# Down projection by seven products of quarters (Strassen's scheme, the form with 15 sums), with the sums of weight quarters made in DRAM by adding DMAs

## Chip, cores and metric

The kernel runs on one core of a Trainium2 chip. The metric is the device time of one execution in microseconds (us), as the median of several runs. Engine names: PE is TensorE, DVE is VectorE, ACT is ScalarE, POOL is GpSimd, SP is SyncE, which here only issues DMAs.

## What is computed

The reference is one decoder layer on 512 tokens of width 1024 in float32: three token mixers, their gated merge, and then a gated feed-forward block. Only the last lines matter here:

```python
D_FF = ((8 * D_MODEL // 3 + 127) // 128) * 128      # 2816
...
h = rmsnorm(x, norm2_g[l])
u = causal_dwconv(h @ ffn_up[l], ffn_conv_w[l], ffn_conv_b[l])
u_gate, u_val = jnp.split(u, 2, axis=-1)
x = x + (jax.nn.gelu(u_gate) * u_val) @ ffn_down[l]
...
return rmsnorm(x, final_g)
```

The down projection is the product with `ffn_down`, a matrix of 2816 rows and 1024 columns.

## The kernel before

Every float32 operand of a matmul is split into a high part (rounded to fp32r by an ACT cast) and a low part (the remainder, by a DVE subtraction), and each product is made of three matmuls: high by high, high by low, low by high. All matmuls are issued at line 77.

The feed-forward block has two stages. In the **up stage** (lines 933 to 949) 44 weight tiles of 128 columns, gate and value in turn, are multiplied with the normalised input; 24 matmuls of 512 columns each. After each pair `glu` (line 921) runs the convolution, the GELU and the gating on DVE and ACT and leaves the result as a pair of pages (`acth`, `actl`), 128 features by 512 tokens. There are 22 such row tiles (`NF`).

In the **down stage** (lines 967 to 1001) the kernel goes over the two halves of the output columns (`hf`). In each, four PSUM banks (`psd`) hold the four token tiles, and 11 weight loads of two row tiles each (`dn_t`) run past them: for each row tile, four token tiles, three matmuls. The activations are stationary, 128 by 128, and the weights move, 128 by 512. The last 2 loads of the first half and the last 4 of the second (`NLAST`) are kept in pages (`load_wp`, line 105), so that the token tiles end one after the other. At the end of a token tile DVE adds the bank to the residual (line 993), ACT makes the sum of squares (line 994), DVE multiplies with the gain (line 996), and in the second half `finish` (line 959) scales with the reciprocal root, whose power is made on POOL (line 867), and stores the result from SP and ACT.

Weights come through `load_w` (line 93): a DMA from SP to a `wr` buffer, the cast to `wh` on ACT (line 101), the remainder `wl` on DVE (line 102). There are three buffers of each of the three kinds. The engines run their instructions strictly in the order in which they were issued to them; a scheduler that simulates a timeline writes that order when the program is built, so it need not be that of the source. Pages (`pg`) are 128 by 512 floats, 58 of them (`NPG`), beside 22 of the second pool (`ag`).

Of the kernel before, what the change touches and what calls it, by code (L numbers as in the profile page):

```python
# [10 lines left out]
F32 = mybir.dt.float32  # L11
F32R = mybir.dt.float32r
AF = mybir.ActivationFunctionType
ALU = mybir.AluOpType
ADD, SUB, MUL, MAX = ALU.add, ALU.subtract, ALU.mult, ALU.max

S = 512
D = 1024
KD = D // 128
NT = S // 128  # L20
DFF = 2816
NF = DFF // 128
EPS = 1e-6
NEG = -1.0e30
NPG = 58
NAT = 22
NWARM = 9
WCOL = 1088
NLAST = (2, 4)
LAM_INIT = 0.2  # L30
GELU_C = 0.7978845608028654
GELU_A = 0.044715
# [14 lines left out]
def build(ctx, tc, A, out):  # L47
# [13 lines left out]
    def pg(name, dt=F32):  # L61
        return page.tile([128, 512], dt, name=name, tag="pg")
# [4 lines left out]
    def bank(name):  # L67
        return psm.tile([128, 512], F32, name=name, tag="mm")

    def abank(name):  # L70
        return psa.tile([128, 512], F32, name=name, tag="at")
# [4 lines left out]
    def mm(ps, a, b, start, stop):  # L76
        PE.matmul(ps, a, b, start=start, stop=stop)  # L77
# [15 lines left out]
    def load_w(ap, n, parts=1):  # L93
        raw = wpool.tile([128, WCOL], F32, name="wr", tag="wr")
        hi = wpool.tile([128, WCOL], F32R, name="wh", tag="wh", bufs=3)
        lo = wpool.tile([128, WCOL], F32R, name="wl", tag="wl", bufs=3)
        with tc.high_priority() if hp[0] else ExitStack():
            for p in range(parts):
                c = slice(n // parts * p, n // parts * (p + 1))
                nc.sync.dma_start(raw[:, c], ap[:, c])  # L100
                SC.copy(hi[:, c], raw[:, c])  # L101
                V.tensor_sub(lo[:, c], raw[:, c], hi[:, c])  # L102
        return hi, lo

    def load_wp(ap):

        raw = wpool.tile([128, WCOL], F32, name="wr", tag="wr")
        nc.sync.dma_start(raw[:, :1024], ap)
        res = []
        for p in range(2):  # L110
            c = slice(512 * p, 512 * (p + 1))
            h = pg("wph", F32R)
            l = pg("wpl", F32R)
            SC.copy(h, raw[:, c])
            V.tensor_sub(l, raw[:, c], h)
            res.append((h, l))
        return res

    def split(src, name, al=None):
        al = al or pg  # L120
        h = al(name + "h", F32R)
        l = al(name + "l", F32R)
        SC.copy(h, src)  # L123
        V.tensor_sub(l, src, h)
        return h, l
# [738 lines left out]
    def rsqrt_act(s1, s0, nm):  # L864
        y = small([128, 1], nm + "y")
        V.tensor_scalar(y, s1, 1.0 / D, s0, op0=MUL, op1=ADD)  # L866
        G.tensor_tensor(y, y, mhalf[:, 0:1], op=ALU.pow)  # L867
        return y
# [43 lines left out]
    def up(wt, name):  # L912
        ps = bank(name)
        mm3(ps, [wt(k) + (h2h[k], h2l[k]) for k in range(KD)])
        return ps

    def up_half(ps, wt, hf):
        c = slice(256 * hf, 256 * (hf + 1))
        mm3(ps[:, c], [wt(k) + (h2h[k][:, c], h2l[k][:, c]) for k in range(KD)])

    def glu(c, psg, psv):
        ug = conv(psg, [col("fw", 44 * j + c) for j in range(3)], col("fb", c))
        uv = conv(psv, [fwh[:, 22 * j + c:22 * j + c + 1] for j in range(3)], fwh[:, 66 + c:67 + c])
        q = pg("gq")
        SC.activation(q, ug, AF.Square)
        V.tensor_scalar(q, q, GELU_A, 1.0, op0=MUL, op1=ADD)
        V.tensor_mul(q, q, ug)
        SC.activation(q, q, AF.Tanh, scale=GELU_C)  # L928
        V.scalar_tensor_tensor(ug, q, 1.0, ug, op0=ADD, op1=MUL)  # L929
        V.tensor_mul(ug, ug, uv)  # L930
        acts.append(split(ug, "act", ag if c < 10 else None))

    acts = []
    order = [i for c in range(NF) for i in (c, NF + c)]
    first_w[1] = up_w(order[1])
    first_w[2] = up_w(order[2])
# [7 lines left out]
    for n in range(3, 2 * NF):  # L944
        w, nxt = nxt, up_w(order[n + 1]) if n + 1 < 2 * NF else None
        ps = up(w, "psu")
        if n % 2:
            glu(n // 2, prev, ps)
        prev = ps

    ss3 = const.tile([128, NT, 2], F32, name="ss3")
    NP = NF // 2
    fgp = []
    for hf in range(2):
        fg = pg("fg")
        nc.sync.dma_start(fg, A["final_g"][512 * hf:512 * (hf + 1)].partition_broadcast(128))
        fgp.append(fg)

    def finish(t):
        z = rsqrt_act(ss3[:, t, 1:2], ss3[:, t, 0:1], "rs3")  # L960
        o = [pg("of") for _ in range(2)]
        SC.activation(o[1], x1[t][1], AF.Copy, scale=z)
        V.tensor_scalar(o[0], x1[t][0], z, None, op0=MUL)
        nc.sync.dma_start(out[128 * t:128 * (t + 1), 0:512], o[0])
        SC.dma_start(out[128 * t:128 * (t + 1), 512:1024], o[1])

    for hf in range(2):
        pst = [bank("psd") for _ in range(NT)]
        held = []

        def dmm(t, k, wh, wl):
            ts_ = slice(128 * t, 128 * (t + 1))
            ah, al = acts[k]
            for j, (a, b) in enumerate(((al, wh), (ah, wl), (ah, wh))):
                mm(pst[t], a[:, ts_], b, k == 0 and j == 0, k == NF - 1 and j == 2)

        nl = NLAST[hf]
        nxt = load_w(A["dn_t"][hf, 0], 1024)
        for p in range(NP - nl):
            hi, lo = nxt  # L980
            if p + 1 < NP - nl:
                nxt = load_w(A["dn_t"][hf, p + 1], 1024)
            else:
                held = [(p, load_wp(A["dn_t"][hf, p])) for p in range(NP - nl, NP)]
            for kk in range(2):
                for t in range(NT):
                    dmm(t, 2 * p + kk, hi[:, 512 * kk:512 * (kk + 1)], lo[:, 512 * kk:512 * (kk + 1)])
        for t in range(NT):
            xx = x1[t][hf]
            for p, w in held:  # L990
                for kk in range(2):
                    dmm(t, 2 * p + kk, *w[kk])
            V.tensor_add(xx, pst[t], xx)
            SC.activation(abank("sqj"), xx, AF.Square, accum_out=ss3[:, t, hf:hf + 1])
            xg = pg("xg")
            V.tensor_mul(xg, xx, fgp[hf])
            x1[t][hf] = xg
            if not hf:
                V.tensor_scalar(ss3[:, t, 0:1], ss3[:, t, 0:1], 1.0 / D, EPS, op0=MUL, op1=ADD)
            else:  # L1000
                finish(t)


def _bucket():
# [12 lines left out]
def layout(i):  # L1017
    f = {k: np.asarray(v) for k, v in i.items()}
    x = f["x"][0]
    w = f["w_in"][0]  # L1020
    o = np.cumsum([0, 1024, 1024, 512, 512, 512, 512, 512, 512, 8, 3072])
    part = [w[:, o[j]:o[j + 1]] for j in range(10)]
    cat = np.concatenate
    A = {}
    A["x"] = np.ascontiguousarray(x)
    A["xT"] = np.ascontiguousarray(x.T.reshape(8, 128, 512).transpose(1, 0, 2))
    A["w_t"] = _tiles(cat([part[0], part[1], part[2], part[3], part[5], part[6], part[9]], axis=1))
    A["wv_d"] = _tiles(part[4], 2, 512)
    A["wv_f0"] = _tiles(cat([part[7][:, :256], part[8]], axis=1), 4, 264)
    A["wv_f1"] = _tiles(part[7][:, 256:], 4, 256)  # L1030
    A["br_r"] = _tiles(f["w_br_rnn"][0])
    for n, w in (("br_d", "w_br_diff"), ("br_f", "w_br_fox")):
        t = _tiles(f[w][0], 4).reshape(4, 2, 128, 512).transpose(0, 2, 1, 3)
        A[n] = np.ascontiguousarray(t).reshape(4, 128, 1024)
    A["w_out"] = np.ascontiguousarray(f["w_out"][0])
    A["up_t"] = _tiles(f["ffn_up"][0])
    d = f["ffn_down"][0].reshape(NF // 2, 2, 128, 2, 512).transpose(3, 0, 2, 1, 4)
    A["dn_t"] = np.ascontiguousarray(d).reshape(2, NF // 2, 128, 1024)
    A["rg_t"] = np.ascontiguousarray(cat([f["rg_w_r"][0], f["rg_w_i"][0]], axis=2))

    def c(v):
        return v.reshape(-1, 128).T

    A["cols"] = np.ascontiguousarray(cat([
        c(f["norm1_g"][0]), c(f["rnn_conv_w"][0]), c(f["rnn_conv_b"][0]), c(f["rg_b_r"][0]), c(f["rg_b_i"][0]),
        c(f["rg_a"][0]), c(f["gate_b"][0]), c(f["norm2_g"][0]), c(f["ffn_conv_w"][0]), c(f["ffn_conv_b"][0]),
        c(f["diff_subln_g"][0])], axis=1))
    A["final_g"] = np.ascontiguousarray(f["final_g"])
    A["rows"] = cat([f["fox_b_f"][0], f["diff_lq1"][0], f["diff_lk1"][0], f["diff_lq2"][0],
                     f["diff_lk2"][0]])  # L1050
    A["rel_bias"] = np.ascontiguousarray(f["rel_bias"])
    A["onehot"] = (np.arange(32)[:, None] == _bucket()[::-1][None, :]).astype(np.float32)
    p = np.arange(128)
    A["mask"] = np.where(p[None, :] <= p[:, None], 0.0, NEG).astype(np.float32)
    A["flip"] = (p[None, :] == 127 - p[:, None]).astype(np.float32)
    return A
# [1 line left out]

# [10 lines left out]
```

## Time and profile before

| | |
|---|---|
| median of 3 runs | 936.99 us (936.97 to 938.68) |
| the profiled execution | 938.8 us, of which the span from first to last instruction is 937.0 us |
| mean granted clock of TensorE | 0.998 of full speed |
| busy time in the span | PE 925.1 us (99%), DVE 633.8 (68%), ACT 482.7 (52%), POOL 95.9 (10%) |
| matmuls of the down stage | 528, from 810.72 us on |

A busy PE only says that a matmul was in flight; the pace is read from the starts of consecutive matmuls. An engine off the critical path costs nothing while it is idle. The profiled execution is one run among several, so a forecast that is summed from its rows is set against its own 938.8 us.

### The profile page before, as it was taken

How to read it: one execution, taken by the hardware profiler on the slowest of the kernel's cores; microseconds unless marked ns; L12 is line 12 of the kernel's file. 1: busy time of each engine (PE TensorE's matmuls, PEld its weight loads, DVE VectorE, ACT ScalarE, POOL GpSimd, SP SyncE). 2: the span in 40 equal slices, each digit the busy share in tenths (PEclk: the TensorE clock that was granted, in tenths of full speed). 3: DMA queues.
4: the chain of work that ended last, by engine and by line, in shares of the span. 5: the costliest groups of instructions: out<-in, count | busy, mean ns of one | idle time of the engine just before them, and what ended most of it. 6: DMA issues, size and time to landing. Idle time of an engine off the chain costs nothing.

```text
span 937.0 us, 11825 instructions
## 1 busy us (share of the span) xinstructions
PE 925.1 (99%) x4363; PEld 771.6 (82%) x4363; DVE 633.8 (68%) x1215; ACT 482.7 (52%) x835; POOL 95.9 (10%) x77
## 2 busy tenths in 40 slices
PE   9999999999999999999999999999999999999997
PEld 6788888998887887888888889888888888888885
DVE  5679797787759778857656734877777777633323
ACT  7577777755465657444454434554444454422212
POOL 0021310200121126321100000000000000000000
PEclk9999999999999999999999999999999999999999
DMA  9522222222322221322245510322322322334112
GB/s 328 173 93 96 80 90 69 69 91 91 107 85 84 97 96 57 105 98 97 73 142 167 189 43 1 113 90 91 111 90 91 111 91 91 113 103 144 45 68 90
DMA packets 31577, 95.14 MB, mean 102 GB/s; under 512 B 3824, under 2 KB 5364, under 8 KB 31520
## 3 DMA queue, kind: packets, MB, share of 16 engines
q1 hardware_dynamic: 30944, 93.35, 29.4%
q10 hardware_dynamic: 576, 1.05, 0.3%
q8 instruction: 34, 0.56, 0.2%
q14 instruction: 23, 0.19, 0.1%
HBM read 92.26 MB, written 2.12 MB: 101 GB/s over the span
## 4 chain that ended last, share of the span: by engine, by line
PE 96%; DVE 2%; issue 1%; ACT 0%; DMA 0%; POOLq 0%; POOL 0%; SPq 0%; ACTq 0%
PE psu L77 26%; PE psgt L77 14%; PE psd L77 12%; PE psbr L77 9%; PE psg L77 6%; PE psv L77 5%; PE psk L77 5%; PE psx L77 5%; PE pswo L77 5%; PE psq L77 4%; PE pss L77 2%; PE pso L77 2%; PE pst L431 1%; DVE wl L102 0%; PE psh L891 0%
## 5 line engine op out<-in xcount | busy, mean ns | idle before, releaser
L102 DVE TENSOR_TENSOR wl<-wr,wh 128x1024 fp32r<-128x1024 f32 (+2 forms) x143 | 175.2, 1225 | 77.4 <-ACT wh L101 62.0
L101 ACT CAST wh<-wr 128x1024 fp32r<-128x1024 f32 (+2 forms) x143 | 146.8, 1028 | 151.3 <-PE psu L77 51.7
L77 PE MATMUL psu<-h2h,wh 128*128 128x512 f32 (+1 forms) x360 | 135.6, 380 | 0.0
L77 PE MATMUL psu<-h2l,wh 128*128 128x512 f32 (+1 forms) x360 | 135.5, 380 | 0.0
L77 PE MATMUL psu<-h2h,wl 128*128 128x512 f32 (+1 forms) x360 | 85.7, 380 | 0.0
L77 PEld LDWEIGHTS psu<-h2l,wh 128*128 128x128 f32 x360 | 67.7, 188 | 12.8
L77 PEld LDWEIGHTS psu<-h2h,wh 128*128 128x128 f32 x360 | 67.7, 188 | 12.7
L77 PEld LDWEIGHTS psu<-h2h,wl 128*128 128x128 f32 x360 | 65.8, 188 | 12.8
L77 PE MATMUL psgt<-xh,wh 128*128 128x512 f32 x192 | 75.6, 394 | 0.0
L77 PE MATMUL psgt<-xl,wh 128*128 128x512 f32 x192 | 75.6, 394 | 0.0
L77 PE MATMUL psd<-wl,acth 128*128 128x512 f32 x128 | 49.8, 389 | 0.0
L77 PE MATMUL psd<-wh,actl 128*128 128x512 f32 x128 | 49.6, 389 | 0.0
L77 PE MATMUL psd<-wh,acth 128*128 128x512 f32 x128 | 49.5, 389 | 0.0
L77 PE MATMUL psgt<-xh,wl 128*128 128x512 f32 x192 | 48.3, 390 | 0.0
L77 PEld LDWEIGHTS psgt<-xh,wh 128*128 128x128 f32 x192 | 36.1, 188 | 7.3
L77 PEld LDWEIGHTS psgt<-xl,wh 128*128 128x128 f32 x192 | 36.1, 188 | 7.2
L77 PEld LDWEIGHTS psgt<-xh,wl 128*128 128x128 f32 x192 | 35.8, 188 | 7.4
L867 POOL TENSOR_TENSOR rs3y<-rs3y,mhalf 128x1 f32<-128x1 f32 x4 | 2.2, 549 | 358.7 <-DVE rs3y L866 358.7
L929 DVE SCALAR_TENSOR_TENSOR u<-gq,u 128x512 f32<-128x512 f32 x22 | 15.2, 692 | 33.2 <-ACT gq L928 33.2
L909 DVE SCALAR_TENSOR_TENSOR u<-psu,cols,u 128x511 f32<-128x511 f32 (+1 forms) x44 | 32.9, 748 | 6.1 <-ACT u L906 5.4
L123 ACT CAST acth<-u 128x512 fp32r<-128x512 f32 x22 | 13.7, 621 | 43.8 <-DVE u L930 43.8
L437 ACT CAST wth<-pst 128x512 fp32r<-128x512 f32 (+3 forms) x48 | 19.6, 423 | 28.8 <-PE pst L431 27.1
(287 smaller groups left out, 2160.9 us busy)
## 6 DMA issues: line engine op xcount, KB each, us to landing
wr<-w_t_in SPq DMA_DIRECT2D x56, 512.0 KB, 3.2
wr<-up_t_in SPq DMA_DIRECT2D x44, 512.0 KB, 3.2
wr<-dn_t_in SPq DMA_DIRECT2D x22, 512.0 KB, 3.2
wr<-br_r_in SPq DMA_DIRECT2D x8, 512.0 KB, 3.2
wr<-w_out_in SPq DMA_DIRECT2D x8, 512.0 KB, 4.0
xraw<-xT_in SPq DMA_DIRECT2D x8, 256.0 KB, 5.2
wr<-wv_d_in SPq DMA_DIRECT2D x8, 256.0 KB, 5.6
xt<-x_in SPq DMA_DIRECT2D x8, 256.0 KB, 5.2
```

The lines of the kernel that those rows point to most:

```text
L77: PE.matmul(ps, a, b, start=start, stop=stop)
L101: SC.copy(hi[:, c], raw[:, c])
L102: V.tensor_sub(lo[:, c], raw[:, c], hi[:, c])
L123: SC.copy(h, src)
L431: PE.transpose(ps[:, 128 * i:128 * (i + 1)], ws[i][:, 128 * j:128 * (j + 1)], ident)
L437: SC.copy(h[:, 128 * j:], ps[:, 128 * j:])
L867: G.tensor_tensor(y, y, mhalf[:, 0:1], op=ALU.pow)
L909: V.scalar_tensor_tensor(u[:, s:], ps[:, :512 - s], w[j], u[:, s:], op0=MUL, op1=ADD)
L929: V.scalar_tensor_tensor(ug, q, 1.0, ug, op0=ADD, op1=MUL)
```

## The change

The three matrices of the down projection are cut into quarters: the activations by even and odd row tiles (11 pairs, `NPAIR`) and by the first and second 256 tokens (`t1`, `t2`), the weights by even and odd row tiles and by the halves of the columns. Seven products of a quarter by a quarter, with sums of quarters as operands, take the place of eight. A product has 11 pairs of operands, two token tiles and three matmuls for each.

The sums on the activation side (`fhs`, `fks`) are made by DVE in the up stage, by `pair_even` and `pair_odd` at the end of each `glu`, and are split into high and low parts later, by `split_pages` in the down stage. The two quarters that are used as they are (`f11`, `f12`) are split at once. The GELU has one DVE instruction less.

The four sums on the weight side (`tsum`) are made in DRAM: `build_sums` is called six times in the up stage, and each time SP issues four copies from DRAM to DRAM and POOL four DMAs that add. The third sum takes the first as an addend, and the fourth the third. Of the seven products, in the order in which they run, the weights are quarter 0, quarter 2, sum 2, sum 0, quarter 3, sum 1, sum 3 (`tsum` counted from 0). Each quarter or sum is loaded in six groups (five of two pairs, one of one), and `ask` keeps three groups ahead. After each product an eviction function (`e1`, `e2`, `e6`, `e5`, `e3`, `e7`, `e4`) adds or subtracts the two banks into the residual. In the last product the last three groups are kept in pages, so that the two token tiles end one after the other. There are 65 pages in place of 58, and the space that the core keeps for DMA descriptors is made smaller.

```diff
-NPG = 58
+NPG = 65
-NLAST = (2, 4)
+NPAIR = NF // 2
+NGRP = 6
+HELD = 3
...
-    def load_wp(ap):
+    def load_wp(ap, n=1024):
...
-        nc.sync.dma_start(raw[:, :1024], ap)
+        nc.sync.dma_start(raw[:, :n], ap)
...
-        for p in range(2):
+        for p in range(n // 512):
...
+    def halves(src, c, al):
+        p = al("ah", F32R)
+        SC.copy(p[:, 0:256], src[:, c])
+        V.tensor_sub(p[:, 256:512], src[:, c], p[:, 0:256])
+        return p
+    t1, t2 = slice(0, 256), slice(256, 512)
+    f11, f12, fhs, fks, f22 = [], [], [], [], []
+    def pair_even(e):
+        f11.append(halves(e, t1, ag))
+        k = pg("fks")
+        V.tensor_sub(k[:, t1], e[:, t1], e[:, t2])
+        fks.append(k)
+    def pair_odd(e, o):
+        f12.append(halves(o, t1, ag))
+        h = pg("fhs")
+        V.tensor_sub(h[:, t1], e[:, t2], o[:, t2])
+        V.tensor_sub(h[:, t2], h[:, t1], e[:, t1])
+        fhs.append(h)
+        k = fks[-1]
+        V.tensor_add(k[:, t2], o[:, t1], h[:, t2])
+        i = len(fhs) - 1
+        if i % 2 == 0:
+            f22.append(pg("f22"))
+        SC.copy(f22[-1][:, 256 * (i % 2):256 * (i % 2 + 1)], o[:, t2])
     def glu(c, psg, psv):
         ug = conv(psg, [col("fw", 44 * j + c) for j in range(3)], col("fb", c))
         uv = conv(psv, [fwh[:, 22 * j + c:22 * j + c + 1] for j in range(3)], fwh[:, 66 + c:67 + c])
         q = pg("gq")
-        SC.activation(q, ug, AF.Square)
-        V.tensor_scalar(q, q, GELU_A, 1.0, op0=MUL, op1=ADD)
-        V.tensor_mul(q, q, ug)
+        SC.activation(q, ug, AF.Square, scale=GELU_A ** 0.5)
+        V.scalar_tensor_tensor(q, q, 1.0, ug, op0=ADD, op1=MUL)
         SC.activation(q, q, AF.Tanh, scale=GELU_C)
         V.scalar_tensor_tensor(ug, q, 1.0, ug, op0=ADD, op1=MUL)
         V.tensor_mul(ug, ug, uv)
-        acts.append(split(ug, "act", ag if c < 10 else None))
+        if c % 2 == 0:
+            even[0] = ug
+            pair_even(ug)
+        else:
+            pair_odd(even[0], ug)
+    even = [None]
+    tsum = [dram.tile([352, 2048], F32, name="tsum%d" % i) for i in range(4)]
+    def quarter(q, g, rows=True):
+        if q < 4:
+            base = A["dn_q"][q:q + 1, 0:1, 0:1]
+        else:
+            base = tsum[q - 4][0:1, 0:1]
+        n = 1024 if g < NGRP - 1 else 512
+        ap = [[2048, n // 16], [1, 2048]] if rows else [[n, 128], [1, n]]
+        return bass.AP(base.tensor, base.offset + g * 64 * 2048, ap), n
+    def build_sums(g):
+        r = slice(64 * g, 64 * g + (64 if g < NGRP - 1 else 32))
+        for i, (a, b) in enumerate(((0, 1), (1, 3), (3, 4), (2, 6))):
+            tc.keep_in_program_order(nc.sync.dma_start(tsum[i][r, :], quarter(a, g)[0]))
+        for i, (a, b) in enumerate(((0, 1), (1, 3), (3, 4), (2, 6))):
+            src = quarter(b, g)[0] if b < 4 else tsum[b - 4][r, :]
+            tc.keep_in_program_order(G.dma_start(tsum[i][r, :], src, accum_op=ADD, max_dma_last_dim=8192))
...
     for n in range(3, 2 * NF):
         w, nxt = nxt, up_w(order[n + 1]) if n + 1 < 2 * NF else None
         ps = up(w, "psu")
+        if n % 6 == 4 and n // 6 < NGRP:
+            build_sums(n // 6)
         if n % 2:
...
-    def finish(t):
-        z = rsqrt_act(ss3[:, t, 1:2], ss3[:, t, 0:1], "rs3")
+    def finish(t, s):
+        z = rsqrt_act(ss3[:, t, s:s + 1], ss3[:, t, 1 - s:2 - s], "rs3")
...
-    for hf in range(2):
-        pst = [bank("psd") for _ in range(NT)]
...
-        for p in range(NP - nl):
...
-                finish(t)
+    half_done = [False] * NT
+    def done(t, hf):
+        xx = x1[t][hf]
+        SC.activation(abank("sqj"), xx, AF.Square, accum_out=ss3[:, t, hf:hf + 1])
+        xg = pg("xg")
+        V.tensor_mul(xg, xx, fgp[hf])
+        x1[t][hf] = xg
+        if half_done[t]:
+            finish(t, hf)
+        else:
+            V.tensor_scalar(ss3[:, t, hf:hf + 1], ss3[:, t, hf:hf + 1], 1.0 / D, EPS, op0=MUL, op1=ADD)
+            half_done[t] = True
+    both = {}
+    def split_pages(name, src, i):
+        h = pg(name, F32R)
+        l = pg(name, F32R)
+        c = t1 if (name, i) == ("s22", NPAIR // 2) else slice(0, 512)
+        SC.copy(h[:, c], src[i][:, c])
+        V.tensor_sub(l[:, c], src[i][:, c], h[:, c])
+        both[name, i] = (h, l)
+    us = [None, None]
+    def add(j, hf, ps):
+        V.tensor_add(x1[j][hf], x1[j][hf], ps)
+    def e1(j, ps):
+        us[j] = pg("us")
+        SC.copy(us[j], ps)
+        add(j, 0, ps)
+    def e2(j, ps):
+        add(j, 0, ps)
+        done(j, 0)
+    def e6(j, ps):
+        V.tensor_add(us[j], us[j], ps)
+        V.tensor_sub(x1[j][1], x1[j][1], us[j])
+    def e5(j, ps):
+        add(j, 1, ps)
+        add(j + 2, 1, ps)
+    def e3(j, ps):
+        add(j, 1, ps)
+        done(j, 1)
+    def e7(j, ps):
+        V.tensor_add(us[j], us[j], ps)
+        add(j + 2, 0, us[j])
+        V.tensor_sub(x1[j + 2][1], x1[j + 2][1], us[j])
+        done(j + 2, 1)
+    def e4(j, ps):
+        add(j + 2, 0, ps)
+        done(j + 2, 0)
+    def first(pages):
+        return lambda i: (pages[i][:, t1], pages[i][:, t2])
+    def second(name, o):
+        return lambda i: tuple(x[:, 256 * o:256 * (o + 1)] for x in both[name, i])
+    def last(i):
+        return tuple(x[:, 256 * (i % 2):256 * (i % 2 + 1)] for x in both["s22", i // 2])
+    prods = [(first(f11), 0, e1, [("shs", fhs, i) for i in range(0, 5)]),
+             (first(f12), 2, e2, [("shs", fhs, i) for i in range(5, 11)]),
+             (second("shs", 1), 6, e6, [("sks", fks, i) for i in range(0, 5)]),
+             (second("shs", 0), 4, e5, [("sks", fks, i) for i in range(5, 11)]),
+             (second("sks", 1), 3, e3, [("s22", f22, i) for i in range(0, 3)]),
+             (second("sks", 0), 5, e7, [("s22", f22, i) for i in range(3, 6)]),
+             (last, 7, e4, [])]
+    seq = [(n, g) for n in range(7) for g in range(NGRP) if n < 6 or g < HELD]
+    ready = []
+    ahead = [0]
+    def ask(m):
+        while ahead[0] < min(m, len(seq)):
+            n, g = seq[ahead[0]]
+            ap, w = quarter(prods[n][1], g, False)
+            ready.append(load_w(ap, w))
+            ahead[0] += 1
+    def pmm(ps, a, i, j, b):
+        ah, al = a(i)
+        c = slice(128 * j, 128 * (j + 1))
+        for x, (l, r) in enumerate(((al, b[0]), (ah, b[1]), (ah, b[0]))):
+            mm(ps, l[:, c], r, i == 0 and x == 0, i == NPAIR - 1 and x == 2)
+    at = 0
+    held = []
+    for n, (a, q, ev, later) in enumerate(prods):
+        pst = [bank("psd") for _ in range(2)]
+        for g in range(NGRP if n < 6 else HELD):
+            ask(at + 3)
+            hi, lo = ready[at]
+            at += 1
+            for i in range(2 * g, min(2 * g + 2, NPAIR)):
+                o = slice(512 * (i % 2), 512 * (i % 2 + 1))
+                for j in range(2):
+                    pmm(pst[j], a, i, j, (hi[:, o], lo[:, o]))
+            k = len(later)
+            for x in later[k * g // NGRP:k * (g + 1) // NGRP]:
+                split_pages(*x)
+            if n == 6 and g + NGRP - HELD >= HELD:
+                ap, w = quarter(7, g + NGRP - HELD, False)
+                held += load_wp(ap, w)
+        with tc.manual_schedule(engines={mybir.EngineType.PE}) if n == 6 else ExitStack():
+            for j in range(2):
+                for i in range(2 * HELD, NPAIR) if n == 6 else ():
+                    pmm(pst[j], a, i, j, held[i - 2 * HELD])
+                ev(j, pst[j])
...
-    d = f["ffn_down"][0].reshape(NF // 2, 2, 128, 2, 512).transpose(3, 0, 2, 1, 4)
-    A["dn_t"] = np.ascontiguousarray(d).reshape(2, NF // 2, 128, 1024)
+    d = f["ffn_down"][0].reshape(NPAIR, 2, 128, 2, 512).transpose(1, 3, 0, 2, 4).reshape(4, NPAIR, 128, 512)
+    g = d[:, :NPAIR - 1].reshape(4, NPAIR // 2, 2, 128, 512).transpose(0, 1, 3, 2, 4)
+    A["dn_q"] = cat([np.ascontiguousarray(g).reshape(4, -1), d[:, NPAIR - 1].reshape(4, -1)],
+                    axis=1).reshape(4, 352, 2048)
...
-    nc = bacc.Bacc("TRN2", target_bir_lowering=False, num_devices=1)
+    nc = bacc.Bacc("TRN2", target_bir_lowering=False, num_devices=1, dynamic_dma_scratch_size=2048)
```

## Rows read from the trace of the kernel before

**Rows 1.** The page: busy time of PE, and its clock in 40 slices

```profile
PE 925.1 (99%) x4363; PEld 771.6 (82%) x4363; DVE 633.8 (68%) x1215; ACT 482.7 (52%) x835; POOL 95.9 (10%) x77
...
PEclk9999999999999999999999999999999999999999
```

**Rows 2.** Chain of waits from 800 on: start, duration, what

```profile
810.89 114.25 PE psd L77 x504
```

**Rows 3.** Timeline of PE: first and last matmul of the down stage (start, duration)

```profile
810.72 0.39 PE L77 MATMUL psd<-wh,actl 128*128 128x512 f32 x1
...
930.18 0.39 PE L77 MATMUL psd<-wph,acth 128*128 128x512 f32 x1
```

**Rows 4.** Windows: busy time by engine (instructions), clock, DMA share, GB/s

```profile
0.00:23.00 23.00, 21.17 (x75) 15.20 (x76) 12.71 (x43) 17.28 (x36) 1.75 (x9) 1.00 0.90 329
586.00:811.00 225.00, 225.00 (x1002) 186.58 (x1001) 168.05 (x233) 110.78 (x148) 0.00 (x0) 1.00 0.30 99
811.00:931.00 120.00, 119.56 (x528) 98.68 (x526) 41.84 (x58) 29.94 (x46) 1.65 (x3) 1.00 0.27 92
```

**Rows 5.** Groups of DVE by form, 811 to 937: busy us, mean ns, idle before

```profile
L102 DVE TENSOR_TENSOR wl<-wr,wh 128x1024 fp32r<-128x1024 f32 x14 | 17.2, 1225 | 39.6 <-ACT wh L101 39.2 <-PE psu L77 0.4
L115 DVE TENSOR_TENSOR wpl<-wr,wph 128x512 fp32r<-128x512 f32 x12 | 7.9, 688 | 9.0 <-ACT wph L114 8.9
L996 DVE TENSOR_TENSOR xg<-x,fg 128x512 f32<-128x512 f32 x8 | 5.5, 692 | 0.3
L993 DVE TENSOR_TENSOR x<-psd,x 128x512 f32<-128x512 f32 x8 | 5.5, 692 | 25.8 <-PE psd L77 25.8
L963 DVE TENSOR_SCALAR of<-xg,rs3y 128x512 f32<-128x512 f32 x4 | 1.9, 486 | 2.7 <-POOL rs3y L867 2.7
...
L926 DVE TENSOR_SCALAR gq<-gq 128x512 f32<-128x512 f32 x1 | 0.4, 419 | 0.0
```

**Rows 6.** Timeline of DVE across the start of the down stage

```profile
809.08 1.53 DVE L909 SCALAR_TENSOR_TENSOR u<-psu,cols,u 128x511 f32<-128x511 f32 x2
810.98 1.23 DVE L102 TENSOR_TENSOR wl<-wr,wh 128x1024 fp32r<-128x1024 f32 x1 [0.36 <-PE psu L77]
...
817.26 0.69 DVE L124 TENSOR_TENSOR actl<-u,acth 128x512 fp32r<-128x512 f32 x1 [0.69 <-ACT acth L123]
```

**Rows 7.** Groups of ACT by form, 811 to 937

```profile
L101 ACT CAST wh<-wr 128x1024 fp32r<-128x1024 f32 x13 | 13.7, 1053 | 39.2 <-PE psd L77 34.0 <-issue 5.2
L114 ACT CAST wph<-wr 128x512 fp32r<-128x512 f32 x12 | 7.0, 619 | 11.2 <-DMA wr<-dn_t_in 11.2
```

**Rows 8.** Waits, 816 to 937: us in total, times, longest

```profile
DVE wl L102 <- ACT wh L101: 39.2, 13, 6.1
```

**Rows 9.** Groups of DVE by form, whole span: a remainder 256 columns wide

```profile
L438 DVE TENSOR_TENSOR wtl<-pst,wth 128x256 fp32r<-128x256 f32 x12 | 5.0, 418 | 2.6 <-ACT wth L437 2.5
```

**Rows 10.** The page's DMA issues: KB each, median us from issue to landing

```profile
wr<-dn_t_in SPq DMA_DIRECT2D x22, 512.0 KB, 3.2
```

**Rows 11.** Timeline of POOL from 560 on

```profile
571.49 0.55 POOL L867 TENSOR_TENSOR rs2y<-rs2y,mhalf 128x1 f32<-128x1 f32 x1 [12.16 <-DVE rs2y L866]
916.06 0.55 POOL L867 TENSOR_TENSOR rs3y<-rs3y,mhalf 128x1 f32<-128x1 f32 x1 [344.02 <-DVE rs3y L866]
```

**Rows 12.** Timeline of SP's issues, 560 on and 779 on

```profile
587.28 192.64 SPq L100 DMA_DIRECT2D wr<-up_t_in  x37
...
779.59 0.33 SPq L100 DMA_DIRECT2D wr<-up_t_in  x1
```

**Rows 13.** Timeline of PE: first matmul of the last up tile

```profile
805.28 0.39 PE L77 MATMUL psu<-h2h,wh 128*128 128x512 f32 x1
```

**Rows 14.** Timeline of the kernel's end

```profile
930.60 0.69 DVE L993 TENSOR_TENSOR x<-psd,x 128x512 f32<-128x512 f32 x1 [2.59 <-PE psd L77]
...
933.71 0.34 ACTq L965 DMA_DIRECT2D y_out<-of  x1
```

**Rows 15.** Groups of POOL, whole span: two of one size

```profile
L671 POOL TENSOR_TENSOR z<-z 128x512 f32<-128x512 f32 x8 | 17.4, 2175 | 61.6 <-DVE z L667 61.6
...
L600 POOL TENSOR_TENSOR cl<-xc,ch 128x512 fp32r<-128x512 f32 x8 | 11.3, 1418 | 37.9 <-ACT ch L599 37.9
```

More of the change, by code (lines that the diff above doesn't have):

```diff
@@ L930, in glu @@
         V.tensor_mul(ug, ug, uv)
-        acts.append(split(ug, "act", ag if c < 10 else None))
-    acts = []
+        if c % 2 == 0:
[20 more added lines that the diff above has]
+            tc.keep_in_program_order(G.dma_start(tsum[i][r, :], src, accum_op=ADD, max_dma_last_dim=8192))
     order = [i for c in range(NF) for i in (c, NF + c)]
@@ L951, in build @@
     ss3 = const.tile([128, NT, 2], F32, name="ss3")
-    NP = NF // 2
     fgp = []
@@ L965, in finish @@
         SC.dma_start(out[128 * t:128 * (t + 1), 512:1024], o[1])
-    for hf in range(2):
-        pst = [bank("psd") for _ in range(NT)]
[L969 to L978, printed above, removed]
-        for p in range(NP - nl):
[L980 to L1000, printed above, removed]
-                finish(t)
```

## The prediction

> **What bounds the kernel now.** I read the page's busy times first. PE is busy in 99% of the span, and its granted clock stands at 9 tenths or more in every slice [rows 1], so there is no throttled stretch to win back. The chain of waits then says what ends last: in the last 137 us it is PE on `psd`, without a break, from 810.89 on [rows 2]. The timeline gives the pace: the first matmul of the down projection starts at 810.72 and the last, the 528th, at 930.18 [rows 3]. That is 119.46 us over 527 steps, 226.7 ns a matmul. The windows by stage show what lies beside it: in the up stage (586 to 811) PE has no idle time, DVE is busy in 168 of 225 us and the DMA engines for 0.30; in the down stage DVE has 41.84 of 120 us and DMA 0.27 [rows 4]. So the stage is worth what its matmuls are worth, and whoever takes matmuls away moves the end, as long as DVE, ACT and the loads, which have to work faster afterwards, keep up.
>
> **The change part by part.** *Matmuls.* Before, 22 row tiles x 4 token tiles x 2 halves x 3 terms = 528. After, 7 products of 11 pairs x 2 token tiles x 3 terms = 462. Operand shapes and their order (low by high, high by low, high by high, a new stationary block each time) stay, so I keep the 226.7 ns: 66 x 0.2267 = 14.96 us less. A product is 66 matmuls = 14.96 us; a group of weights (two pairs) is 12 = 2.72 us, half of the 5.44 us that it had.
>
> *DVE and ACT in the down stage.* By the rows [rows 5]: 33 wide weight remainders x 1.225 = 40.4; 11 of half width x 0.688 = 7.6; 28 remainders of activation sums (`split_pages`) x 0.688 = 19.3; in the seven evictions 30 operations of 512 columns (2, 4, 4, 4, 4, 8, 4) x 0.692 = 20.8; `finish` and small ones about 2.8. Sum 91 us of the new 104.7, where it was 42 of 120. To this comes the last `glu`, which in the trace of before keeps DVE from the stage's start to 817.95 [rows 6]: 98 of 104.7. ACT: 33 x 1.053, 39 x 0.619 [rows 7], and about 10 for the rest: 69 us. DVE therefore comes close to PE without passing it, and what counts is order, not sum. In before DVE had 39.2 us of waits for ACT's casts in this stage [rows 8], which shows how much its order is tied to the weight buffers.
>
> There are three `wh`/`wl` buffers, so the cast of group g+2 can start when PE has finished group g-1, and it is needed 5.44 us later. Cast and remainder take 1.05 + 1.23 = 2.3. At the end of a product the eviction stands ahead of the remainder in DVE's queue, since it is issued first and waits for PE: 4 operations are 2.8 us, with the small ones 3.1. So 3.1 + 1.2 = 4.3 of 5.44: no stall, after products 1 to 5 (`e1`, `e2`, `e6`, `e5`, `e3`). After the sixth (`e7`) it is 8 operations: 5.5 + 1.2 = 6.8, a stall of 1.3 us; bounds 0 (the order written by the scheduler puts the remainder in between) and 2.5. At the stage's start the last `glu` does the same: 7.0 us of DVE work, now with ACT's gaps between, against remainders due at 5.44 and 8.16; the work due by 8.16 is about 7.0 + 2 x 1.2 = 9.4, so I take 1.0, bounds 0 (its tail need not be early, as `f12` of the last pair is read 28 us later) and 3. For the other boundaries I take 0, with bounds 0 and 1.3 each.
>
> *Up stage.* In `glu` one TENSOR_SCALAR of 0.42 goes, and the two remainders of a pair (2 x 0.69) give way to six operations of 256 columns; the nearest row for that width is 0.418 [rows 9]: 2.5 - 1.4 - 0.8 = +0.3 us per pair, 3.5 us in the stage on DVE's 168 of 225. PE covers that; without this cover it would cost the 3.5. ACT is level: two casts of 0.62 go, three of some 0.4 come.
>
> *The sums.* Six times, at every sixth weight load of the up stage, SP issues 4 copies within DRAM and POOL 4 adding DMAs, of 512 KB each (the last group half). The trace of before has neither operation. Nearest: a 512 KB load lands after 3.2 us [rows 10]. Queues: POOL has nothing to do from 572 to 916 [rows 11], so nobody stands behind its waits but the next sum and `rs3` at the end. On SP the following loads stand behind the copies. Their lead is long: the last up weights are issued at 779.59 and first used at 805.28 [rows 12, 13], 25.7 us; less 3.2 to land and 2.3 to split, 20 us are left. Four copies one behind the other are 4 x 3.2 = 12.8: hidden. The engines: at a share of 0.90 they moved 329 GB/s, so full is 365 [rows 4]. Per six loads (32.6 us, 11.9 MB at full rate) there are 3.1 MB of loads and 2.1 of copies; adds that read two sources and write one are 4.2 by reads, 9.4 MB in all (79%). Counted with the writes too it is 13.6 MB or 37.3 us, 4.7 us too much each time, 28 in six, less the lead of 20: 8 us of stall as the upper bound of this part. I take 0, since loads of before, too, pass as reads at one rate. In the down stage a load each 2.72 us is 193 GB/s, about half of 365.
>
> *Are the sums there in time?* The first two products read plain quarters; the third, 29.9 us in, is the first that reads a sum, and its last group is wanted on SP near 846. POOL takes the groups one after another from about 587 (the loads of the stage run from there [rows 12]), so a group may take (846 - 587) / 6 = 43 us, 10.8 us per add if they run in series, against 3.2 for a load of that size. [...] The sum goes by 0.
>
> *Tail.* The last matmul starts at 930.18, its eviction 0.4 us later, and the last output DMA is issued at 933.71 [rows 3, 14]. `e4` ends in the same operations, so 0; bounds -0.3 and +0.5.
>
> *Sum.* The profiled execution took 938.8 (span 937.0 and 1.8 around it), which is 1.8 over the median of 936.99. 938.8 - 15.0 + 1.3 + 1.0 = 926.1 for such an execution, and 1.8 less against the median: 924.3. With all small bounds: 921.7 to 929.
>
> **The rivals.**
> *DVE becomes the bound.* For it: 98 of 104.7 us of work, in one queue in order, with a wait for PE at the head of each eviction. Against it: each remainder has 1 to 3 us of slack at the boundaries above. If each of six boundaries costs 1.3 us and the start 3, it is 936.99 - 15.0 + 7.8 + 3 = 932.8, still faster; with half of that, 928.
>
> *The sums are late (slower than before).* Place: SP, at the load of the third product, where all later loads queue behind the wait. It decides from 43 us per group on; at 43 + 12.7/6 = 45 the gain is gone. [...] Chance 0.09.
>
> *The traffic of the sums starves the weight stream* in the up stage, the upper bound above: 924.3 + 8 = 932. For it the count with writes, against it the lead. Chance 0.06.
>
> *The change doesn't do what it says,* because PE's pace on pages that hold two halves side by side is another one: 5% either way is 5.2 us of the stage, 919 or 929.5. Against it: the down stage of before reads two kinds of weights (wide tiles and single pages), and its pace is one. Chance of under 921: 0.06.
>
> **How the numbers follow.** My forecast (921 to 928, the likeliest 924.3, told as 924.5) has 0.62; DVE as bound (928 to 933) 0.17; starved stream 0.06; late sums 0.09; better pace 0.06. The range of 8 in 10 takes forecast and DVE as bound and some of the stream: 921 to 933. A measurement of this kernel tells about 0.2% (1.9 us) from no change. Faster by more is all but the late sums and a little of the other two slow cases: 0.88; slower 0.09; within 0.03.
>
> **What would show it.** In the changed profile: 462 `psd` matmuls at 226.7 ns; a stage of 104.7 us plus gaps; the gaps, if any, within 10 us of its start and 5 us after the sixth product, released by DVE's `wl`. DVE near 9 tenths there. No PE idle time in the up stage, adds landing in under 10 us. Wrong would be: PE waiting at the third product for a DMA (late sums), PE gaps in the up stage released by DMA (starved stream), or gaps at every product boundary (DVE as bound).

## The result, and the profile after

The changed kernel takes 922.25 us (922.16 to 922.63, 4 runs) against 936.98 for the kernel before; the ratio is 0.9845, 95% interval [0.9824, 0.9866]. That is 14.7 us less. Forecast were 924.5 and a range of 921 to 933.

The page of the changed kernel: PE is as busy as before, the DMA engines are far busier in the up stage, and a new queue (q0, POOL's) carries the adds. The last four rows are DMA issues: KB each, median us from issue to landing.

```profile
PE 907.9 (99%) x4297; PEld 757.6 (82%) x4297; DVE 679.3 (74%) x1295; ACT 516.3 (56%) x892; POOL 114.7 (12%) x101
...
PEclk9999999999999999999999999999999999999999
DMA  9522222222322221223126361576887662255573
...
q0 software_dynamic: 1792, 11.54, 7.0%
...
tsum<-dn_q_in SPq DMA_DIRECT2D x20, 512.0 KB, 7.3
wr<-tsum SPq DMA_DIRECT2D x20, 512.0 KB, 4.0
...
tsum<-dn_q_in POOLq DMA_DIRECT2D x10, 512.0 KB, 8.4
tsum<-tsum POOLq DMA_DIRECT2D x10, 512.0 KB, 6.7
```

The timeline of PE, first and last matmul of the down stage, answers to [rows 3]:

```profile
808.37 0.39 PE L79 MATMUL psd<-wh,ah 128*128 128x512 f32 x1
...
912.87 0.39 PE L79 MATMUL psd<-wph,s 128*128 128x512 f32 x1
```

104.50 us lie between the starts of 462 matmuls: 226.7 ns each, to the last digit the pace of before, and so without any gap. The stage is 14.96 us shorter, as summed. The windows answer to [rows 4]: the up stage, and the down stage with the tail's first instructions.

```profile
586.00:808.00 222.00, 222.00 (x981) 183.82 (x980) 169.82 (x249) 109.92 (x154) 15.54 (x20) 1.00 0.63 185
808.00:913.00 105.00, 105.00 (x465) 86.82 (x463) 83.49 (x117) 62.19 (x93) 2.70 (x3) 1.00 0.57 183
```

PE has no idle time in either. DVE does 83.5 of 105 us in the down stage.

The two profiled executions differ by more than the change, 938.8 - 922.2 = 16.6 us. The timelines split it: the down stage begins 2.35 us earlier (808.37 against 810.72), it is 14.96 shorter, and from its last matmul to the end of the span pass 7.5 us where it was 6.8. The 2.35 are no part of the change. Timeline of PE at the start of the kernel before, and then of the changed one, the same first four products:

```profile
5.85 2.08 PE L77 MATMUL psv<-wh,xh 128*128 128x512 f32 x4 [0.49 <-ACT wh L101]
7.72 1.91 PE L77 MATMUL psv<-wh,xl 128*128 128x512 f32 x4
```

```profile
5.89 1.19 PE L79 MATMUL psv<-wh,xh 128*128 128x512 f32 x4 [0.52 <-ACT wh L103]
6.92 1.08 PE L79 MATMUL psv<-wh,xl 128*128 128x512 f32 x4
```

In this execution of before the first 11 real matmuls went at about half pace, 0.43 us a step, which put everything behind them 2.2 us later. Of the 14 executions profiled in this study five began so (before, and the runs `e4_before_pages`, `e5_dve_half`, `e7_adds_six`, `e10_dve_seven`; 8 to 11 matmuls), old and new kernels alike. The trace's record of the granted clock begins, at full speed, at 9.9 to 10.8 us in these five (10.73 in before) and at 4.1 to 6.3 us in the nine others (5.54 in the changed kernel), and in all 14 the step falls from 0.43 to 0.23 us around that moment, also where it comes during the warming matmuls on zeros that stand ahead (nine of them take 4.02 us in the changed kernel and 3.44 in `e1_after_again`). Ahead of it there is no record, and the windows print 1.00 there: a lower clock until then is my estimate from the step, and not shown.

A second difference of that kind lies in the middle of the kernel, which the change left alone. After a stop of PE of 2.24 us, which every one of the 14 executions has, the clock falls to one half for 3.4 us in ten of them (in the profiled executions of before and of the changed kernel alike) and stays full in four (`e1_after_again`, `e7_adds_six`, `e9_adds_twelve`, `e12_warm_ten`): the longest `psq` matmul takes 628 to 632 ns in the ten and 499 in the four, and the windows print 0.50 from 356 to 358 us in before and from 354 to 357 in the changed kernel. The windows of the changed kernel, and then of `e1_after_again`, the same program; the column before the DMA share is the granted clock:

```profile
353.00:358.00 5.00, 4.91 (x15) 3.91 (x16) 4.96 (x10) 3.81 (x10) 4.88 (x4) 0.66 0.36 137
```

```profile
353.00:358.00 5.00, 4.89 (x22) 4.12 (x23) 4.96 (x10) 4.54 (x11) 4.87 (x4) 1.00 0.38 138
```

It puts the down stage 1.6 us later (808.37 against 806.79). A slice of the page is some 23 us long, so such a stretch still prints as a 9 in PEclk. The two together make 3.8 us, which no change of the kernel explains; below, lengths of the down stage are compared for that reason, from its first matmul to its last.

### The profile page after: what moved, and what is told of

It is laid out like the page before. It is cut to its first block, busy times and chain, and to the rows that moved or that the text cites. A ratio compares the mean times of both kernels' runs of the same rounds, so it can differ in the third digit from the quotient of the medians.

```text
span 920.4 us, 11975 instructions
## 1 busy us (share of the span) xinstructions
PE 907.9 (99%) x4297; PEld 757.6 (82%) x4297; DVE 679.3 (74%) x1295; ACT 516.3 (56%) x892; POOL 114.7 (12%) x101
## 3 DMA queue, kind: packets, MB, share of 16 engines
q0 software_dynamic: 1792, 11.54, 7.0%
HBM read 123.98 MB, written 25.19 MB: 162 GB/s over the span
## 4 chain that ended last, share of the span: by engine, by line
PE 96%; DVE 2%; issue 0%; ACT 0%; DMA 0%; SPq 0%; POOLq 0%; POOL 0%
PE psu L79 26%; PE psgt L79 14%; PE psd L79 11%; PE psbr L79 9%; PE psg L79 6%; PE psv L79 5%; PE psk L79 5%; PE psx L79 5%; PE pswo L79 5%; PE psq L79 4%; PE pss L79 2%; PE pso L79 2%; PE pst L433 1%; DVE wl L104 0%; DMA wr<-wv_d_in 0%
## 5 line engine op out<-in xcount | busy, mean ns | idle before, releaser
L104 DVE TENSOR_TENSOR wl<-wr,wh 128x1024 fp32r<-128x1024 f32 (+2 forms) x166 | 201.2, 1214 | 82.6 <-ACT wh L103 41.5
L103 ACT CAST wh<-wr 128x1024 fp32r<-128x1024 f32 (+2 forms) x166 | 168.4, 1016 | 152.0 <-PE psu L79 64.5
L911 DVE SCALAR_TENSOR_TENSOR u<-psu,fwh,u 128x511 f32<-128x511 f32 (+1 forms) x44 | 32.7, 744 | 0.0
L440 DVE TENSOR_TENSOR wtl<-pst,wth 128x512 fp32r<-128x512 f32 (+3 forms) x48 | 22.6, 482 | 13.3 <-ACT wth L439 13.0
L960 ACT ACTIVATE gq<-gq 128x512 f32<-128x512 f32 x22 | 13.9, 633 | 26.2 <-DVE gq L959 26.2
L79 PE MATMUL psv<-wh,xh 128*128 128x512 f32 (+2 forms) x96 | 27.8, 320 | 0.5 <-ACT wh L103 0.5
L541 ACT ACTIVATE sc<-sc,nm 128x128 f32<-128x128 f32 (+3 forms) x32 | 17.9, 559 | 18.3 <-DVE nm L539 18.2
L79 PE MATMUL psv<-wh,xl 128*128 128x512 f32 (+2 forms) x96 | 27.8, 320 | 0.0
```

The costliest lines, as they stand in the source:

```text
L440: V.tensor_sub(l[:, 128 * j:], ps[:, 128 * j:], h[:, 128 * j:])
L541: SC.activation(sc[:, :n], sc[:, :n], AF.Exp, bias=nm, accum_out=sm_)
L911: V.scalar_tensor_tensor(u[:, s:], ps[:, :512 - s], w[j], u[:, s:], op0=MUL, op1=ADD)
```

## The experiments

**The changed kernel again** (`e1_after_again`), beside before on one chip.

> The changed kernel once more, beside the kernel before on one chip. My theory (66 matmuls of 226.7 ns less, all else hidden): 14 to 15 us less than before, about 922.3 us. The rival that the first measurement owed part of its gain to the start of the profiled executions (their first twelve matmuls went at half pace before and at full pace after, 2.2 us) gives 12.5 us or less here.

Measured: 920.81 us (920.63 to 924.27) against 936.55 (15 runs), ratio 0.9843 [0.9822, 0.9864]; 15.7 us less, a little more than I expected. The gain is not that of one lucky start. The excess is no gain of the change: this profiled execution (920.63) has neither the slow start nor the stretch at half clock near 353 us, while its down stage takes 104.49 us and its tail 7.6, as in the first measurement. By the two parts that the change touches, 14.96 less for the stage and 0.7 more for the tail, it is worth 14.2 us; what the medians show beyond that hangs on which executions were caught.

**66 matmuls left out of the kernel before** (`e2_less66`).

```diff
+            cut = hf == 0 and t < 3
             for j, (a, b) in enumerate(((al, wh), (ah, wl), (ah, wh))):
-                mm(pst[t], a[:, ts_], b, k == 0 and j == 0, k == NF - 1 and j == 2)
+                if cut and j == 0:
+                    continue
+                mm(pst[t], a[:, ts_], b, k == 0 and j == (1 if cut else 0), k == NF - 1 and j == 2)
```

> The kernel before, with 66 of its 528 matmuls of the down projection left out: the term low part of the activations by high part of the weights, for three token tiles of the first column half. Nothing is added. My theory, that the gain is the number of matmuls alone: 14.96 us less than before, the same as the changed kernel within 1 us. If the changed kernel still hides a cost of its sums or evictions, this one is faster than it by that cost (2 us or more).

Measured: 921.63 us (919.96 to 922.25), ratio 0.9836 [0.9818, 0.9853]. Its timeline of PE:

```profile
808.51 0.39 PE L77 MATMUL psd<-wl,acth 128*128 128x512 f32 x1
...
913.00 0.39 PE L77 MATMUL psd<-wph,acth 128*128 128x512 f32 x1
```

104.49 us, the stage of the changed kernel (104.50) within the rounding of the view, with half of its DVE work (41.7 us against 83.5). So in this stage all that the seven products need besides matmuls is hidden. Behind it the changed kernel is 0.7 us longer (7.5 us from the last matmul to the end, here 6.8).

**No sums** (`e3_no_sums`): the call of `build_sums` is taken out, and `quarter` reads quarter `q % 4`.

> The changed kernel without the copies and the adding DMAs; the products that should read a sum read a plain quarter of the same size in its place. My theory, that the traffic of the sums is hidden: the same time as the changed kernel within 1 us. The rival, that the traffic holds up the weight stream of the up stage, or the end of the kernel: faster by 2 us or more.

Measured: 921.62 us (920.56 to 921.94), ratio 0.9836 [0.982, 0.9853], beside 920.81 for the changed kernel on that chip. Windows by stage:

```profile
586.00:808.00 222.00, 222.00 (x981) 183.81 (x980) 170.00 (x249) 109.85 (x154) 0.00 (x0) 1.00 0.31 100
808.00:913.00 105.00, 105.00 (x465) 86.95 (x464) 83.56 (x117) 62.13 (x94) 2.69 (x3) 1.00 0.59 183
```

The sums double the DMA share of the up stage (0.63 against 0.31) and cost no time in either stage.

**More pages for the kernel before** (`e4_before_pages`): `NPG` 65 and the smaller descriptor space.

> The kernel before with 65 pages and the smaller space for DMA descriptors, nothing else. My theory: 937 us, the same as before within 1 us. The rival, that the 2.4 us by which the profile of the changed kernel was already ahead when its down stage began come from the pages: 2 us less than before.

Measured: 936.52 us (11 runs) against 936.55, ratio 1.0 [0.999, 1.001]. The pages are worth nothing by themselves.

**More DVE work in the down stage** (`e10_dve_seven`, `e5_dve_half`, `e6_dve_full`): in the loop over groups, behind the matmuls, for 7, 20 and 39 groups,

```diff
+            if g == 1:                  # 20: g % 2 == 0; 39: always
+                V.tensor_sub(abank("dum"), fgp[0], fgp[1])
             k = len(later)
```

> The changed kernel with one more subtraction of 512 columns on DVE in each product (seven, 4.8 us of work). The run with 20 showed that DVE stalls PE with 98 us of work in the stage. My present theory, that the loop buffer, load, cast, remainder has 1 to 3 us of room at the boundaries: the stage stays at 104.5 or grows by less than 1.5. The rival, that there is no room at all and every addition shows: 3 to 5 us.

> The changed kernel with one more subtraction of 512 columns on DVE (into a free PSUM bank, read by nobody) at every second weight group of the down stage: 20 of them, 13.8 us of DVE work, which takes DVE from 84 to 98 us of the stage's 104.5. My theory, that DVE has slack that its order can use: the stage stays within 1 us of 104.5. The rival, that DVE is already the bound by its order: the stage grows by 3 to 8 us.

> As the run before, but at every weight group: 39 subtractions, 26.9 us, which takes DVE to 111 us of work in a stage of 104.5. My theory: DVE now sets the pace, the stage grows by 6 to 10 us. The rival by order: by 10 us or more.

One run each:

| subtractions | DVE work added | length of the down stage | growth |
|---|---|---|---|
| 0 | 0 | 104.5 us | |
| 7 | 4.8 us | 105.9 | 1.4 |
| 20 | 13.8 | 113.9 | 9.4 |
| 39 | 26.9 | 122.9 | 18.4 |

My expectation for seven held, barely; those for 20 and 39 fell, and the rival that order counts was right, with more than the 3 to 8 us that it gave for 20. With 20 the sum of DVE's work, 84 + 14 = 98 us, would fit the old stage. The timeline of PE with 20 shows where it stops:

```profile
827.53 0.50 PE L79 MATMUL psd<-wl,ah 128*128 128x512 f32 x1 [1.31 <-DVE wl L104]
851.61 0.50 PE L79 MATMUL psd<-wl,shs 128*128 128x512 f32 x1 [0.63 <-DVE wl L104]
857.71 1.22 PE L79 MATMUL psd<-wh,shs 128*128 128x512 f32 x2 [3.06 <-ACT wh L103]
917.99 0.50 PE L79 MATMUL psd<-wpl,s 128*128 128x512 f32 x1 [1.36 <-DVE wpl L117]
```

The longest wait is for a cast, and the timeline of ACT says what that cast waited for; then the remainders on DVE, and the issue of the load:

```profile
856.61 1.04 ACT L103 CAST wh<-wr 128x1024 fp32r<-128x1024 f32 x1 [2.59 <-DMA wr<-tsum]
```

```profile
845.47 1.22 DVE L104 TENSOR_TENSOR wl<-wr,wh 128x1024 fp32r<-128x1024 f32 x1
...
850.34 1.22 DVE L104 TENSOR_TENSOR wl<-wr,wh 128x1024 fp32r<-128x1024 f32 x1
...
854.49 1.22 DVE L104 TENSOR_TENSOR wl<-wr,wh 128x1024 fp32r<-128x1024 f32 x1
```

```profile
851.59 10.41 SPq L102 DMA_DIRECT2D wr<-tsum  x4
```

A group lasts 2.72 us on PE, but here the remainders come 4 to 5 us apart, as subtractions of both kinds stand between them. A `wr` buffer is free when its remainder is done, the next load into it waits on SP for that, and it lands 3.2 to 4.9 us later (median 3.4): the remainder of 850.34 ends at 851.56, SP issues the load at 851.59, and the cast of 856.61 waits for it. So a delay on DVE comes back as a late DMA three groups on, by the ring of three buffers; the other three waits, 3.3 us in sum, are for remainders directly. Then the clock adds to it; windows of PE behind the stop:

```profile
857.00:858.00 1.00, 0.29 (x1) 0.63 0.84 279
858.00:860.00 2.00, 2.00 (x5) 0.50 0.39 143
860.00:862.00 2.00, 2.00 (x9) 0.83 0.56 217
```

After 3.06 us without a matmul the granted clock was 0.50 for some 3.4 us by these windows, and PE did 5 matmuls in 2 us where it does 9, which cost some 1.5 us. PE's waits sum to 6.4 us here, the stage grew by 9.4; the rest, about 1.5 us, lies in the steps around each stop, which are 0.1 to 0.3 us longer than 0.227. With seven there is no stretch at half clock, and two waits of 0.3 us for remainders make 1.4 us in the same way.

The added subtractions wait for nothing, so the scheduler may place them where it likes, and it bunches them: with 20, nine start between 847.3 and 859.2, around the longest stop; with seven, three start between 844.8 and 846.0, and the two waits end at 856.2 and 865.1. The runs price bursts on DVE; what the same work would cost if it were spread evenly they do not show.

**More adds** (`e7_adds_six`, `e8_adds_eight`, `e9_adds_twelve`): in `build_sums`,

```diff
+            for _ in range(2):          # six: range(3 if i == 3 else 1); twelve: range(3)
-            tc.keep_in_program_order(G.dma_start(tsum[i][r, :], src, accum_op=ADD, max_dma_last_dim=8192))
+                tc.keep_in_program_order(G.dma_start(tsum[i][r, :], src, accum_op=ADD, max_dma_last_dim=8192))
```

> The changed kernel with the last add of each group made three times (six adds in place of four; the sum itself is then another). The chain of adds of a group goes from about 28 to about 43 us, just at the limit of 43 that I worked out before the result. My theory (a sum is late only from that limit on): the last adds end about 825 us, no stall or one below 3 us. The rival, that adds cost the weight stream: PE gaps in the up stage.

> The changed kernel with every add made twice, one behind the other (eight in place of four). The chain of a group goes to 50 to 55 us, over the limit. My theory: POOL falls behind by 18 us or more a group, the last sum is there near 880 to 900 us, and PE stands still in the third product for 30 to 50 us. The rival, that the sums have much more room than I reckoned: no stall.

> The changed kernel with every add made three times. Eight adds took 46 us a group, stood at a DMA share of 0.89 in the up stage and cost nothing, because the first group begins at 570, not 587, and the last is a half: the limit is (846 - 570) / 5.5 = 50 us a group. Twelve adds should take 65 to 72 us. My theory (late sums): the last sum is there at 930 to 960 us, PE stands still in the third product, and the time is 1000 to 1035 us, with no PE gap in the up stage. The rival, that adds take second place behind loads without end and the weight stream starves first: PE gaps in the up stage.

Measured, one run each: 922.57, 923.36 and 1023.17 us; down stages of 104.5, 105.3 and 207.1. Six held as to the stall; the last add is issued at 771.8, where I had the end at 825, since the groups followed each other some 35 us apart and not 43. For eight I was wrong by a wide margin: 0.8 us and no stop worth the name, though POOL needed some 47 us for a group. The window of the up stage and the last add of that run:

```profile
586.00:808.00 222.00, 222.00 (x981) 183.89 (x980) 169.83 (x249) 109.59 (x154) 29.97 (x38) 1.00 0.89 231
```

```profile
831.92 0.77 POOL L990 DMA_DIRECT2D tsum<-tsum  x1 [5.53 <-DMA tsum<-tsum]
```

The limit of 43 us came from a first group at 587 and six whole ones. The trace has POOL's first add at 570, and the last group is a half, so the limit is (846 - 570) / 5.5 = 50. Twelve adds are beyond it, and there the mechanism is what I had described. POOL's last add, and PE's stops:

```profile
956.07 0.77 POOL L990 DMA_DIRECT2D tsum<-tsum  x1 [4.63 <-DMA tsum<-tsum]
```

```profile
900.23 1.22 PE L79 MATMUL psd<-wh,shs 128*128 128x512 f32 x2 [50.81 <-ACT wh L103]
948.37 1.22 PE L79 MATMUL psd<-wh,shs 128*128 128x512 f32 x2 [42.55 <-ACT wh L103]
```

94 us of waiting for the last two groups of the third product, and none in the up stage, where PE was busy for 222.00 of 222 us at a DMA share of 0.89 too: in these runs late sums come long before a starved weight stream. With eight adds the loads of up weights landed after 6.2 us in the middle and 15.0 at most (3.7 and 7.4 in the changed kernel), and the lead of 20 us covered it.

**The GELU of before in the changed kernel** (`e11_gelu_back`): the two lines of `glu` taken back to their three.

> The changed kernel with the GELU of the kernel before: a TENSOR_SCALAR of 0.42 us and a product in place of one instruction, 22 times. [...] My theory: the end does not move (within 1 us apart from the start of the execution), and POOL's adding instructions stay near 0.78 us with a few longer ones, by up to 0.42. [...]

Measured: 921.8 us in one run, a down stage of 104.5. POOL's adding instructions (duration in ns, min/median/max) in this run, and then in the changed kernel:

```profile
L990 POOL DMA_DIRECT2D tsum<-tsum x12: 768/778/876, 575.2 to 748.7; - x12
```

```profile
L989 POOL DMA_DIRECT2D tsum<-tsum x12: 771/778/804, 575.2 to 749.1; - x12
```

The longest of these twelve became 0.07 us longer, the other twelve take 1.10 us at most in both runs, the adds land after 8.5 and 6.0 us at the median (8.4 and 6.7 in the changed kernel), and the last add is issued at the same time. The longest is also the only one of the 24 that met a TENSOR_SCALAR; timelines of POOL and of DVE:

```profile
722.97 0.88 POOL L990 DMA_DIRECT2D tsum<-tsum  x1 [5.93 <-DMA tsum<-tsum]
```

```profile
723.36 0.42 DVE L959 TENSOR_SCALAR gq<-gq 128x512 f32<-128x512 f32 x1
```

One meeting and 0.1 us do not show that a TENSOR_SCALAR on DVE holds up POOL's adds, and it would have no weight here.

**Ten warming matmuls** (`e12_warm_ten`): `NWARM` 10 in place of 9.

> The changed kernel with ten in place of nine matmuls on zeros ahead of the first product, so that PE is busy up to the moment when the first weights are ready (5.36 before, 5.85 needed). In some executions of all kernels the first twelve real matmuls run at half pace, which costs 2.2 us. If the gap of 0.5 us has to do with it: a median 0.5 to 1.5 us under that of the changed kernel (920.8 to 922.3) and a smaller spread. If not: no change.

Measured: 922.25 us (920.82 to 922.93), ratio 0.9847 [0.9831, 0.9864]. No change is seen, and the run does not test what it was meant to: the gap did not close. Timeline of PE:

```profile
1.35 3.79 PE L172 MATMUL pwarm<-warm 128*128 128x512 bf16 x10 [1.35 <-POOL warm L169]
5.95 1.19 PE L79 MATMUL psv<-wh,xh 128*128 128x512 f32 x4 [0.82 <-ACT wh L103]
```

In this execution ten warming matmuls took 3.79 us where nine took 4.02 in the changed kernel: the last of them went at full pace and ended early, and PE stood still for 0.82 us all the same. Four runs between 920.82 and 922.93 would not show an effect of 0.5 us either. The pace of the first matmuls went with the moment at which the trace's record of the clock begins, in all 14 executions; what decides that moment stays open. No run points to a version that is faster than the changed kernel.

## Why the prediction was right

*Matmuls, 14.96 us.* Right, to the hundredth, and shown by itself: the kernel before with 66 matmuls fewer has the same stage. The pace on pages that hold two halves is the 226.7 ns of before, so the rival of another pace is out.

*DVE close to PE, order counts.* Right in kind. The sum was 91 us and 7 for the last `glu`, 98. Added up by their durations the operations that start in the stage make 91.5 us (two of the 33 wide remainders and the end of the last eviction lie outside it); the windows say 83.5, nearer 8 tenths than the 9 that I named, since operations of 0.69 us that follow each other on DVE start 0.60 apart. But the two stalls that I summed, 1.3 us behind the sixth product and 1.0 at the start, did not come: each term was at its lower bound of 0. For the first the reason is the order, as the bound had it. Timeline of DVE in the changed kernel, behind the sixth product:

```profile
897.88 0.69 DVE L1076 TENSOR_TENSOR us<-us,psd 128x512 f32<-128x512 f32 x1 [1.31 <-PE psd L79]
898.48 1.22 DVE L104 TENSOR_TENSOR wl<-wr,wh 128x1024 fp32r<-128x1024 f32 x1
899.62 0.68 DVE L1076 TENSOR_TENSOR us<-us,psd 128x512 f32<-128x512 f32 x1
```

The scheduler put the remainder behind the first of the eight operations of `e7`. At the start of the stage it did the same, and two remainders stand between the operations of the last `glu`:

```profile
812.54 0.69 DVE L962 TENSOR_TENSOR u<-u 128x512 f32<-128x512 f32 x1
813.15 1.22 DVE L104 TENSOR_TENSOR wl<-wr,wh 128x1024 fp32r<-128x1024 f32 x1
814.28 0.42 DVE L944 TENSOR_TENSOR fhs<-u 128x256 f32<-128x256 f32 x1
```

Without these two terms the forecast is 922.0, and with the tail's 0.7 it is 922.7 (922.25 measured). That it agrees to half a us is luck: executions of one program differ by 3.6 us (920.63 to 924.27) for reasons outside the change, and the median of the second measurement, 920.81, lies just under the range that began at 921.

*No throttled stretch.* I read that from the nines of PEclk [rows 1]. The profiled execution of before has one, 3.4 us at half clock behind 355 us (0.50 in the window from 356 to 358), which the slices are too long to show; it touches neither the stage nor the sum.

*DVE becomes the bound (0.17).* It did not, but the room is smaller than the 21 us of idle time suggest: seven operations, 4.8 us, part of them in bursts, already cost 1.4.

*Up stage, at nothing.* Right: 222.00 of 222 us busy, with the sums and without them. I had reckoned the traffic at 79% by reads, with two reads for an add; the share is 0.63, and a second read is not shown: the HBM reads on the page grow by one byte for each byte added (23.07 MB more from four adds to twelve, which move 23.07 MB more).

*Sums in time.* Right. The 0 rested on a time for an add that was my estimate and that no run shows; what the runs showed in its place are adds that land in 6.7 to 8.4 us at the median (I named under 10; the longest took 10.3), against 10.8 for the limit, and about 28 us for a group, from the first copy at 603.7 to the last add, issued at 625.6 and landed some 6.5 later. The limit was wrong (50 and not 43). For the late sums (0.09) no run shows POOL held up by DVE: with DVE busy for 169.8 of 222 us, POOL's adding instructions took 0.78 us at the median and 1.10 at most.

*Tail, 0 with a bound of +0.5.* Off by a little: 7.5 us against 6.8. It lies behind the last output DMA, issued 4.0 us before the span ends (916.4 to 920.4) where it was 3.3 [rows 14]. The runs with adding DMAs have 3.6 to 4.1 there, the others 3.3 to 3.5; what the program does in that time the profile does not show, and the cause stays open.

## What to carry to other kernels

Where PE ran without a gap, matmuls taken away were worth their count times the pace read from the trace (66 x 0.2267 = 14.96 us), and a run that merely leaves them out tells whether the rest is hidden (104.49 us against 104.50). Idle time of an engine that feeds a short ring of buffers was no measure of its room: DVE had 21 us idle, and 4.8 us of work more, in bursts, cost 1.4 us, because a late remainder held up PE directly, and with 13.8 us more it returned as a late load too. DMAs that compute lay under a long stage of matmuls at no cost (222.00 of 222 us busy with and without them); for another kernel, work out when the last of them is wanted and what stands behind it in each queue.

## What the runs showed of the hardware

- An adding DMA from DRAM to DRAM took about 64 us of the 16 engines for 11.54 MB (7.0% of 920.4), 179 GB/s, and twice the adds took 131.8 us for 23.07 MB (14.3% of 921.4). By the packets recorded in the up stage of the changed kernel (586 to 808) the adds moved 9.44 MB in 51.7 us of the 16 engines, 182 GB/s, and the plain copies within DRAM as much in 25.5 us, 370 GB/s: a ratio of 2.0. Whether a second read is the reason no run here shows: the HBM reads on the profile's page grow by one byte for each byte added (123.98 MB with four adds, 147.05 with twelve, which move 23.07 MB more).
- A stop of PE of 3.06 us was followed by some 3.4 us at a granted clock of 0.50 (`e5_dve_half`), which cost some 1.5 us more, so the stop cost half as much again as its length. A stop of 2.24 us near 353 us was followed by 3.4 us at half clock in ten of 14 profiled executions, at a cost of 1.6 us, and by none in four.
- The warming matmuls and up to 11 real ones behind them ran at 0.43 us a step, and at 0.23 from about the moment at which the trace's record of the granted clock begins, at 4.1 to 6.3 us in nine executions and at 9.9 to 10.8 in five (2.2 us later from there on). The windows give 1.00 ahead of that moment, where the trace has no record of the clock.
